# Weight products of 512 columns issued as halves of 256 columns

## The chip, the cores and the metric

The kernel runs on one core of a Trainium2 chip. The metric is the device time of one execution in microseconds (us). Before the change the median of three runs is 2204.62 us (2203.36 to 2204.85).

The core's engines work side by side: TensorE (PE in the profile) multiplies matrices, and its loading of the stationary operand, the weight load, is listed apart as PEld. VectorE is DVE, ScalarE is ACT, GpSimd is POOL, and SyncE (SP) issues most of the DMAs. A matmul writes to PSUM, an accumulation memory of banks that hold 512 float32 columns on each of 128 partitions. All other operands are in SBUF.

## The reference

The reference is a decoder trunk of two layers over 256 tokens of width 2048, in float32. Each layer is a mixer and a SwiGLU FFN, with an RMSNorm before and after each and the result added to the residual stream.

```python
for layer in range(DEPTH):                      # DEPTH = 2
    y = rms_norm(h, g[0])
    if layer % 2 == 0:
        y = sb_gla_mixer(y, w_in, w_gate_up, b_gate, gla_norm_gain, w_out)   # w_in 2048 x 6160, w_out 2048 x 2048
    else:
        y = s5_mixer(y, ..., w_glu)                                          # w_glu 2048 x 4096
    h = h + rms_norm(y, g[1])
    y = swiglu_ffn(rms_norm(h, g[2]), w_ffn_in[layer], w_ffn_out[layer])     # 2048 x 11264 and 5632 x 2048
    h = h + rms_norm(y, g[3])
```

The first mixer has stick-breaking attention and gated linear attention (GLA) between its two projections. The second has a diagonal state-space layer (S5), a GELU and a gated linear unit (GLU). Most of the arithmetic is in the six large weight matrices, and these are what the change is about.

## The kernel before, in words

**How a weight product is made.** The 256 tokens are two token blocks of 128. A weight matrix is cut into column blocks of 512, and each column block into units of 256 rows, that is two k-tiles of 128 rows. For a column block and a token block, TensorE sums over all k-tiles into one PSUM bank of 128 tokens x 512 columns. The stationary operand is 128 x 128 activations (k-tile by tokens), the moving operand 128 x 512 weights.

**The split into high and low parts.** To come close to float32 with TensorE's faster float32 type (F32R in the code), both operands are split into a high part, rounded to F32R, and a low part, the remainder. Three products of a k-tile are summed: high activation by high weight, high by low, low by high. In the code these are `xh`, `xl` for the activations and `hi`, `lo` for the weights; their tiles are whi and wlo for the weights and xh/xl, ah/al, og and os for the activations. A unit has two k-tiles, so a unit and a token block have six products. They are issued in the method `products` (lines 203 to 205), one k-tile after the other.

**Raw products.** The first eight units of the GLU aren't split. Their weights go in as float32 (`lo` is None, line 198), two products to a unit.

**How the weights come.** The class `Stream` has a plan of all weight chunks in the order of use (the method `plan`). A chunk is 512 rows x 512 columns, 1 MB, loaded by one DMA on SP's queue into one of 3 buffers (tile wraw). `convert` makes one unit from half a chunk: ScalarE copies 128 x 1024 elements into whi, and VectorE subtracts to get wlo; 5 buffers of each. `next` hands out units and converts a few ahead (the argument `ahead`, 3 or 4).

**The loops.** `linear` goes over column blocks, and in each over units; for each unit it calls `products` for token block 0 and then 1, and then `pump`, which issues some other work (attention, GLA, preparation of S5) between units, by a budget of estimated nanoseconds. After the last unit of a column block, ScalarE and VectorE read the two banks (`evac`). `pairwise` is the same for two column blocks by turns. The order in each engine's queue is the order in which the program calls, since the schedule is manual.

**Other matmuls that the prediction speaks of.** Line 734 is a small product of the GLA gate: 128 x 16 weights, F32R, moving operand 256 columns, 48 products in one accumulation. Line 810 is a float32 product of 128 x 128 by 128 columns in the GLA's levels. Lines 923 and 924 are float32 products of the attention with 256 and 128 columns. Line 1233 is a float32 product with 32 stationary columns in the preparation of S5; lines 480, 337 and 612 are transposes on TensorE.

Of the kernel before, what the change touches and what calls it, by code (L numbers as in the profile page):

```python
# [159 lines left out]
class Kern:  # L160
# [31 lines left out]
    def products(self, ps, acts, tb, u, part):  # L192
        hi, lo = part
        mm = self.nc.tensor.matmul
        if lo is None:
            for kk in range(2):
                k = 2 * u + kk
                mm(ps, lhsT=self.whole[k][:, tb * 128:(tb + 1) * 128], rhs=hi[:, kk, :], start=(k == 0), stop=(k == len(acts) - 1))  # L198
            return
        for kk in range(2):  # L200
            k = 2 * u + kk
            xh, xl = (a[:, tb * 128:(tb + 1) * 128] for a in acts[k])
            mm(ps, lhsT=xh, rhs=hi[:, kk, :], start=(k == 0), stop=False)  # L203
            mm(ps, lhsT=xh, rhs=lo[:, kk, :], start=False, stop=False)  # L204
            mm(ps, lhsT=xl, rhs=hi[:, kk, :], start=False, stop=(k == len(acts) - 1))  # L205


    def linear(self, blocks, acts, evac, opening=None, mid=None, hooks=None, spare=None):
# [497 lines left out]
    def gla(self, rs):  # L706
# [86 lines left out]
        yield from self.need(256)  # L793
        mix = self.got.pop(256)
        yield from products(S[1], mix, mix, 0, 128, lambda o, p: nc.vector.tensor_copy(o, p))
        for li, b in enumerate((64, 32, 16, 8, 4, 2, 1)):
            yield from self.need(2 * b + 1)
# [805 lines left out]
```

## Time and profile before

| What | Value |
|---|---|
| Median of the runs | 2204.62 us (2203.36 to 2204.85, 3 runs) |
| The profiled execution's own time | 2204.35 us |
| Its span, from the first to the last instruction | 2202.6 us |
| TensorE busy | 2159.6 us (98%), 10672 matmuls |
| Weight loads (PEld) | 1741.4 us (79%), 10672 |
| VectorE busy | 1319.5 us (60%) |
| ScalarE busy | 974.3 us (44%) |
| Mean granted clock of TensorE | 0.996 |
| DMA | 457.42 MB, mean 208 GB/s |

The page of the profile gives busy times, the groups of instructions and the chain of work that ended last. A row of a group reads: line, engine, operation, output and inputs, shapes, count, then the busy time and the mean of one in ns, then the idle time of the engine before them and what ended it. Successive matmuls overlap in the profile, so the mean duration of one is longer than the distance between two starts. A row of the timeline reads: start in us, length in us, engine, line, operation, output and inputs, shape, count; equal neighbours are merged into one row. A matmul's shape is written as weight rows x weight columns and then the moving operand. A row for one line of the program gives the shortest, the median and the longest duration in ns.

### The profile page before, as it was taken

The numbers are of one execution on the slowest core, as the hardware profiler recorded it, in microseconds if no ns is written. First come the engines' busy times: TensorE is split into PE (matmuls) and PEld (weight loads), VectorE is DVE, ScalarE is ACT, GpSimd is POOL, SyncE is SP. The second block draws the span as 40 slices with busy tenths as digits, with TensorE's granted clock in tenths as the row PEclk, the third lists the DMA queues.
The fourth block names the chain that finished last, engine by engine and source line by source line (L and its number), as shares of the span: only waits on it lengthen the run. The fifth ranks groups of instructions, "written<-read, shape, count | busy, mean of one in ns | idle before, by whom it ended". The sixth has DMA issues, their size and how long they took to land.

```text
span 2202.6 us, 26942 instructions
## 1 busy us (share of the span) xinstructions
PE 2159.6 (98%) x10672; PEld 1741.4 (79%) x10672; DVE 1319.5 (60%) x1913; ACT 974.3 (44%) x1222; POOL 7.1 (0%) x14
## 2 busy tenths in 40 slices
PE   8999999999999999999998899999999999999998
PEld 6888888788888888777786678878888888888886
DVE  4675654667777877875456864564544454444445
ACT  5454544463454444334344254464434444433433
POOL 0000000000000000000000000000000000000000
PEclk9999999999999999999999999999999999999999
DMA  7554454555687778988769865645555555555553
GB/s 230 171 176 156 159 173 155 206 190 175 202 268 236 241 221 267 300 275 275 238 214 349 305 209 185 213 170 176 195 183 191 191 173 190 174 206 174 191 172 134
DMA packets 261742, 457.42 MB, mean 208 GB/s; under 512 B 22736, under 2 KB 66016, under 8 KB 260720
## 3 DMA queue, kind: packets, MB, share of 16 engines
q1 hardware_dynamic: 260896, 450.99, 62.0%
q0 software_dynamic: 720, 4.72, 0.6%
q8 instruction: 83, 1.36, 0.2%
q14 instruction: 43, 0.35, 0.0%
HBM read 425.26 MB, written 30.41 MB: 207 GB/s over the span
## 4 chain that ended last, share of the span: by engine, by line
PE 94%; DVE 3%; ACT 1%; DMA 1%; issue 0%; SPq 0%; DVEq 0%; ACTq 0%
PE lin L203 29%; PE lin L205 29%; PE lin L204 29%; PE lin L198 1%; PE big L480 1%; DVE h L65 1%; DVE X L65 0%; PE big L810 0%; DVE wlo L65 0%; ACT xh L65 0%; PE big L1233 0%; PE big L205 0%; PE big L204 0%; PE big L203 0%; DVE xl L65 0%
## 5 line engine op out<-in xcount | busy, mean ns | idle before, releaser
L65 DVE TENSOR_TENSOR wlo<-wraw,whi 128x1024 fp32r<-128x1024 f32 x705 | 850.3, 1222 | 591.1 <-ACT whi L65 588.8
L65 ACT CAST whi<-wraw 128x1024 fp32r<-128x1024 f32 x705 | 725.3, 1051 | 670.7 <-PE lin L205 609.2
L203 PE MATMUL lin<-whi,xh 128*128 128x512 f32 x1984 | 790.6, 398 | 3.4 <-ACT xh L65 3.4
L204 PE MATMUL lin<-wlo,xh 128*128 128x512 f32 x1984 | 785.1, 396 | 3.0 <-DVE wlo L65 2.9
L205 PE MATMUL lin<-whi,xl 128*128 128x512 f32 x1984 | 784.9, 396 | 0.9 <-DVE xl L65 0.9
L203 PEld LDWEIGHTS lin<-whi,xh 128*128 128x128 f32 x1984 | 374.9, 189 | 91.2 <-ACT xh L65 4.0
L204 PEld LDWEIGHTS lin<-wlo,xh 128*128 128x128 f32 x1984 | 374.8, 189 | 90.4 <-DVE wlo L65 6.0
L205 PEld LDWEIGHTS lin<-whi,xl 128*128 128x128 f32 x1984 | 374.5, 189 | 88.7 <-DVE xl L65 2.2
L203 PE MATMUL lin<-whi,ah 128*128 128x512 f32 x680 | 270.0, 397 | 0.0
L205 PE MATMUL lin<-whi,al 128*128 128x512 f32 x680 | 268.9, 395 | 0.0
L204 PE MATMUL lin<-wlo,ah 128*128 128x512 f32 x680 | 268.9, 395 | 0.0
L203 PEld LDWEIGHTS lin<-whi,ah 128*128 128x128 f32 x680 | 128.1, 188 | 30.8 <-issue 1.2
L205 PEld LDWEIGHTS lin<-whi,al 128*128 128x128 f32 x680 | 128.1, 188 | 30.3
L204 PEld LDWEIGHTS lin<-wlo,ah 128*128 128x128 f32 x680 | 128.1, 188 | 30.0
L65 DVE SCALAR_TENSOR_TENSOR a<-lin,rs,a 128x512 f32<-128x512 f32 x44 | 31.0, 746 | 67.3 <-PE lin L205 67.3
L65 ACT ACTIVATE a<-lin,rs 128x512 f32<-128x512 f32 x44 | 27.9, 684 | 92.2 <-PE lin L205 92.2
L65 DVE TENSOR_TENSOR yg<-lin,yg 128x512 f32<-128x512 f32 x30 | 19.9, 687 | 52.1 <-PE lin L205 52.1
L65 ACT ACTIVATE junk<-yg 128x512 f32<-128x512 f32 x24 | 15.2, 632 | 74.1 <-DVE yg L65 74.1
L65 ACT CAST ah<-big 128x1024 fp32r<-128x1024 f32 x22 | 22.3, 1015 | 56.2 <-PE big L480 56.2
L65 DVE TENSOR_TENSOR al<-big,ah 128x1024 fp32r<-128x1024 f32 x22 | 26.9, 1223 | 17.1 <-ACT ah L65 17.1
L65 ACT ACTIVATE xh<-big,gT 128x128 fp32r<-128x128 f32 (+1 forms) x80 | 24.3, 394 | 21.5 <-PE big L337 16.9
L65 DVE SCALAR_TENSOR_TENSOR xl<-big,gT,xh 128x128 fp32r<-128x128 f32 (+1 forms) x80 | 24.5, 371 | 13.6 <-ACT xh L65 13.6
(323 smaller groups left out, 1287.1 us busy)
## 6 DMA issues: line engine op xcount, KB each, us to landing
wraw<-w_ffn_in SPq DMA_DIRECT2D x176, 1024.0 KB, 5.1
wraw<-w_ffn_out SPq DMA_DIRECT2D x88, 1024.0 KB, 5.5
wraw<-w_in SPq DMA_DIRECT2D x47, 1024.0 KB, 5.0
wraw<-w_glu SPq DMA_DIRECT2D x32, 1024.0 KB, 5.7
wraw<-w_out SPq DMA_DIRECT2D x16, 1024.0 KB, 5.1
e_d<-ed SPq DMA_DIRECT2D x64, 144.0 KB, 5.9
et<-e_d SPq DMA_DIRECT2D x16, 576.0 KB, 6.3
win_d<-win SPq DMA_DIRECT2D x32, 256.0 KB, 6.6
```

The lines of the kernel that those rows point to most:

```text
L65: return f(*a, **k)
L198: mm(ps, lhsT=self.whole[k][:, tb * 128:(tb + 1) * 128], rhs=hi[:, kk, :], start=(k == 0), stop=(k == len(acts) - 1))
L203: mm(ps, lhsT=xh, rhs=hi[:, kk, :], start=(k == 0), stop=False)
L204: mm(ps, lhsT=xh, rhs=lo[:, kk, :], start=False, stop=False)
L205: mm(ps, lhsT=xl, rhs=hi[:, kk, :], start=False, stop=(k == len(acts) - 1))
L480: nc.tensor.transpose(p[:, tb, i, :], a[:, tb, i * 128:(i + 1) * 128], self.ident)
```

## The change

The six products of a unit and a token block are no longer issued k-tile by k-tile over the whole bank. They are collected in a list in the same order, and issued for the left 256 columns of the bank and then for the right 256. Two products stay whole, 512 columns wide: the first of an accumulation, which starts it, and the last, which stops it. Every half has a matmul instruction of its own with its own weight load. The raw products (line 198) stay as they are, and no other line is touched.

```diff
+        terms = []
         for kk in range(2):
             k = 2 * u + kk
             xh, xl = (a[:, tb * 128:(tb + 1) * 128] for a in acts[k])
-            mm(ps, lhsT=xh, rhs=hi[:, kk, :], start=(k == 0), stop=False)
-            mm(ps, lhsT=xh, rhs=lo[:, kk, :], start=False, stop=False)
-            mm(ps, lhsT=xl, rhs=hi[:, kk, :], start=False, stop=(k == len(acts) - 1))
+            terms += [(xh, hi[:, kk, :]), (xh, lo[:, kk, :]), (xl, hi[:, kk, :])]
+        first, last = u == 0, 2 * u + 2 == len(acts)
+        if first:
+            x, w = terms.pop(0)
+            mm(ps, lhsT=x, rhs=w, start=True, stop=False)
+        final = terms.pop() if last else None
+        for c in (slice(0, 256), slice(256, 512)):
+            for x, w in terms:
+                mm(ps[:, c], lhsT=x, rhs=w[:, c], start=False, stop=False)
+        if last:
+            x, w = final
+            mm(ps, lhsT=x, rhs=w, start=False, stop=True)
```

## The prediction, made before the changed kernel was run

> **What bounds the kernel now.** I read the page from its engine line to the chain of waits and the groups, then TensorE's waits, then one long stretch of products in the timeline.
>
> ```profile
> span 2202.6 us, 26942 instructions
> PE 2159.6 (98%) x10672; PEld 1741.4 (79%) x10672; DVE 1319.5 (60%) x1913; ACT 974.3 (44%) x1222; POOL 7.1 (0%) x14
> ...
> PE 94%; DVE 3%; ACT 1%; DMA 1%; issue 0%; SPq 0%; DVEq 0%; ACTq 0%
> ...
> L65 DVE TENSOR_TENSOR wlo<-wraw,whi 128x1024 fp32r<-128x1024 f32 x705 | 850.3, 1222 | 591.1 <-ACT whi L65 588.8
> L65 ACT CAST whi<-wraw 128x1024 fp32r<-128x1024 f32 x705 | 725.3, 1051 | 670.7 <-PE lin L205 609.2
> L203 PE MATMUL lin<-whi,xh 128*128 128x512 f32 x1984 | 790.6, 398 | 3.4 <-ACT xh L65 3.4
> ```
>
> TensorE is busy for 98% of the span and makes 94% of the chain that ended last. The conversions of the weights (VectorE 1.22 us, ScalarE 1.05 us for each unit of 128x1024) feed it, and they sit idle for 591 and 671 us. So whatever changes TensorE's pace in the weight products changes the time almost one to one. The 398 ns of a product is not its price, because products overlap; the price is the distance between starts:
>
> ```profile
> 1811.87 0.48 PE L203 MATMUL lin<-whi,xh 128*128 128x512 f32 x1
> 1812.18 0.39 PE L204 MATMUL lin<-wlo,xh 128*128 128x512 f32 x1
> ...
> 1856.33 0.39 PE L205 MATMUL lin<-whi,xl 128*128 128x512 f32 x1
> ```
>
> ```profile
> L203 PE MATMUL lin<-whi,xh 128*128 128x512 f32 x64 | 25.4, 396 | 0.0
> L204 PE MATMUL lin<-wlo,xh 128*128 128x512 f32 x64 | 25.3, 395 | 0.0
> L205 PE MATMUL lin<-whi,xl 128*128 128x512 f32 x64 | 25.3, 395 | 0.0
> ```
>
> The second fence groups the stretch from 1811.87 us to 1856.57 us: 192 products and no idle time. From the second of them (1812.18) to the last (1856.33) are 190 distances in 44.15 us, or **232.4 ns for a product of 512 columns**. The granted clock was 1.00 there, and over most of the span:
>
> ```profile
> 1811.87:1856.57 44.70, 44.70 (x195) 36.27 (x194) 20.99 (x20) 18.64 (x19) 0.00 (x0) 1.00 0.56 188
> 465.00:1195.00 730.00, 730.00 (x3388) 586.92 (x3386) 505.58 (x862) 310.59 (x366) 0.29 (x1) 1.00 0.77 246
> ```
>
> (Columns: length, busy time of TensorE, of its weight loads, of VectorE, ScalarE and GpSimd, then granted clock, DMA share, GB/s.) VectorE's busiest long stretch, 465 to 1195 us, is 69% busy.
>
> **The change: how many instructions.** From the plan in the code: 96 units for w_in, 32 for w_out, 2 x 264 for the two FFNs, 56 for the GLU beside its 8 raw ones, 712 in all; times 2 token blocks and 6 products is 8544, which at 232.4 ns is 1986 us of the span. Left whole are the first product of each accumulation (92 column blocks x 2, less the 4 that begin raw: 180) and the last (184). So 8544 - 364 = **8180 products are split**: TensorE executes 10672 + 8180 = 18852 matmuls and as many weight loads. Every nanosecond that two halves cost over one whole is 8.2 us.
>
> **The price of a half** isn't in the trace: no matmul there has 256 columns of F32R data against 128 weight columns. These rows come closest (they write f32 for both types; the code tells which is F32R and which F32).
>
> ```profile
> 45.73 0.28 PE L734 MATMUL big<-xl,wlr_split 128*16 128x256 f32 x1
> ...
> 50.84 0.28 PE L734 MATMUL big<-xl,wlr_split 128*16 128x256 f32 x1
> ```
>
> ```profile
> L734 PE MATMUL big<-xl,wlr_split x16: 276/277/280, 45.7 to 50.8; 128*16 128x256 f32 x16
> ```
>
> The gate's low-rank product: F32R, 256 columns, each with its own weight load, accumulating into the same columns as a half will, but only 16 weight columns. One in three reads xl; sixteen of these span 15 x 3 = 45 distances in 5.11 us, or 113.6 ns. Two make 227.2, which is 5.2 ns *less* than 232.4.
>
> ```profile
> 118.42 1.79 PE big L810 x16
> ```
>
> ```profile
> L810 PEld LDWEIGHTS big<-qd,de x112: 187/192/193, 118.0 to 197.4; 128*128 128x128 f32 x112
> L810 PE MATMUL big<-qd,de x112: 273/276/276, 118.3 to 197.5; 128*128 128x128 f32 x112
> ```
>
> F32 of 128 columns lasts 276 ns against the 277 of L734, so it streams as long as a half, and here each has a full load of 128 weight columns. Sixteen take 1.79 us in the chain: 111.9 ns each. So a full load (192 ns long by itself) can hide under a stream of this length, and 111.9 is the fastest pace at which loads of this size are seen to follow one another. That is the lower bound: 2 x 111.9 - 232.4 = **-8.6 ns** a split.
>
> ```profile
> 1249.41 20.84 PE L198 MATMUL lin<-wraw,y 128*128 128x512 f32 x48 [0.63 <-DMA e<-e_d]
> ```
>
> ```profile
> L198 PE MATMUL lin<-wraw,y x64: 592/593/697, 1249.4 to 1281.8; 128*128 128x512 f32 x64
> L923 PE MATMUL big<-sqT,skT x16: 377/380/383, 239.9 to 338.9; 128*128 128x256 f32 x16
> ```
>
> ```profile
> 239.95 0.59 PE L923 MATMUL big<-sqT,skT 128*128 128x256 f32 x2
> 240.38 0.39 PE L924 MATMUL big<-sqT,skT 128*128 128x128 f32 x2
> ```
>
> What an instruction costs beside its columns: 593 - 380 = 213 ns is the stream of 256 F32 columns, 426 that of 512. The pace of L198 is (20.84 - 0.59) / 47 = 431 ns, 5 more; the pace of L923 is 0.43 / 2 = 215, 2 more. So **2 to 5 ns per instruction**, with 128 weight columns each time. I take 2.5, nearer the short instruction, since 2.5 also leaves room for the one late start inside L198's 48.
>
> The upper bound: 256 F32 columns stream in 213 ns, so 512 F32R columns, which last 393 to 396 ns against 380, stream in 213 or a little more. Were all of the 232.4 - 213 = 19.4 ns a price of the instruction, a split would cost **+19.4 ns**.
>
> The choice: of 232.4 I put 2.5 on the instruction and the rest on the 512 columns (0.449 ns each, where L734's are (113.6 - 2.5) / 256 = 0.434). Then a half is 117.4, two are 234.9, and a split costs **+2.5 ns**. I prefer it to L734's -5.2 because L734 lacks the 128 weight columns, and because a stream that costs less per column when it is short needs a reason that no row gives.
>
> The Trainium skill (TensorE: Matmul & The Clock Gate, Part 1, "Wait — 56ns, not 53.3ns?") gives a matmul N / 2.4 GHz plus about 2.5 ns, so 215.7 ns for 512 columns and, as an estimate from it, 109.2 for 256. The trace does not agree on the first (232.4, at a granted clock of 1.00), and the measurement decides. By that page's fixed term alone the change costs 8180 x 2.5 ns, 20 us.
>
> The same skill (Perfetto Trace Analysis, "Identifying the Most-Contended Engine") judges TensorE by the share of the time in weight-load slices, which speaks against this change: 79% now, and an estimate of 149% after, from 8180 more loads of 188 ns. L810's row shows that 192 ns slices follow each other every 111.9 ns, so slices overlap, and over 100% is no proof of a bound here.
>
> **The rest.**
>
> ```profile
> PE lin L204 <- DVE wlo L65: 2.9, 5, 0.8
> ```
>
> ```profile
> q8 instruction: 83, 1.36, 0.2%
> ...
> wraw<-w_ffn_in SPq DMA_DIRECT2D x176, 1024.0 KB, 5.1
> ```
>
> The first product with the low part starts up to 116 ns earlier after its unit's first one. That meets a late VectorE in 5 places (2.9 us in all): +0.6 us at most. whi is last read by the last product as before; wlo's last reading is the eleventh half of twelve, 116 ns later than now, under VectorE's 591 us of idle time: nothing. The last product stays whole, so what evacuates a bank waits for the same instruction. No load of weights is moved on SP's or POOL's queue. The instructions themselves come by DMA: 1.36 MB for 21344 of TensorE's is 64 bytes each, so 16360 more are 1.05 MB, 64 packets; no row shows TensorE waiting for them, and I take 0. If that cover were gone, each could cost what a load takes to land, 5.1 us: 326 us.
>
> Sum: 8180 x 2.5 ns = 20.5, + 0.6 = 21 us, against the profiled execution's own 2204.35 us (span 2202.6 and 1.75 around it; the median of the runs shown is 2204.62): **2225 us**. With 1 to 5 ns a split: 2212 to 2246.
>
> **Rivals.**
>
> *Short streams are cheaper (faster).* L734's pace holds with 128 weight columns too: 8180 x -5.2 = -43 us, **2162**. For it: the one row with F32R data of 256 columns; full loads can follow at 111.9, so they needn't stop it. Against it: 16 weight columns. It decides as soon as a half stays under 116.2 ns; at the floor of 111.9 it gives -70 us, 2134.
>
> *No change.* A half is just half, within 0.5 ns a split: **2204**. It needs the instruction's 2 to 5 ns to be offset by a cheaper stream.
>
> *The excess belongs to the switch of weights.* Part or all of the 19.4 ns comes with each change of 128 weight columns; a half then takes up to 126 ns: +159 us, **2363**, and half of it 2284. For it: 16 weight columns in L734 leave only 113.6 - 106.5 = 7.1 ns of excess, half of L923's 213 being 106.5. Against it are these rows:
>
> ```profile
> 863.75 0.40 PE L205 MATMUL lin<-whi,xl 128*128 128x512 f32 x1
> 864.07 0.64 PE L1233 MATMUL big<-et 128*32 128x128 f32 x16
> ```
>
> ```profile
> 864.07 0.38 PEld L1233 LDWEIGHTS big<-et 128*32 128x32 f32 x16 [0.36 <-PE lin L204]
> ```
>
> Beside the product at 863.75 no weights were loaded (the loads were idle for 0.36 us before 864.07), and it still lasted 0.40 us, like the others. So a load that runs beside a product doesn't seem to be what stretches it.
>
> *It doesn't do what it says*: the loads of a half can't keep up, or instructions come late, as priced above. Nothing in the trace speaks for it.
>
> **How the numbers follow.** Forecast 0.42; cheaper short streams 0.32; no change 0.12; the switch of weights 0.12; the last 0.02. A measurement of this kernel tells 0.2%, 4.4 us, from no change. Slower 0.42 + 0.12 + 0.02 less 0.01 for the low end of the forecast = 0.55; same 0.13; faster 0.32. The predicted time is 2225; its own range is 2212 to 2246. The range of 8 in 10 runs from 2150, below L734's price and above the floor of 2134, to 2320, most of the way to a whole excess at each switch.
>
> **What would show it.** In the changed profile: 18852 matmuls; the stretch of two FFN column blocks that took 44.70 us takes 45.2 by the forecast, 43.7 by L734's price, 48.3 by the switch; a half's distance is 117.4, 113.6 or 126 ns. VectorE's and ScalarE's busy times stay at 1319 and 974 us, and the waits of L198, L810 and the other stages stay as they are. I am wrong if a half takes under 116 ns, or if new idle time of TensorE appears within a unit.

## The result, and the profile after

The changed kernel takes **2238.56 us** (median of 4 runs, 2237.77 to 2241.25) against 2204.49 us before (4 runs): a ratio of 1.0158, 95% interval 1.0140 to 1.0175, so 34 us slower. The forecast was 2225 us, slower; its own range was 2212 to 2246.

The page of the changed kernel, in the same order as before; line 212 now issues the halves, 208 and 215 the first and last whole products.

```profile
span 2237.0 us, 43302 instructions
PE 2193.5 (98%) x18852; PEld 2142.3 (96%) x18852; DVE 1319.6 (59%) x1913; ACT 974.7 (44%) x1222; POOL 7.1 (0%) x14
...
q8 instruction: 147, 2.41, 0.4%
...
PE 40%; DVE 1%; ACT 1%; issue 0%; DVEq 0%; ACTq 0%
...
L65 DVE TENSOR_TENSOR wlo<-wraw,whi 128x1024 fp32r<-128x1024 f32 x705 | 850.0, 1222 | 614.8 <-ACT whi L65 609.9
L212 PE MATMUL lin<-wlo,xh 128*128 128x256 f32 x3968 | 1106.8, 282 | 3.1 <-DVE wlo L65 2.9
```

18852 matmuls, as counted. TensorE's busy time grew by 33.9 us and the span by 34.4: the loss lies within TensorE's own stream. Its idle time is 43.5 us (2237.0 - 2193.5) after 43.0. VectorE and ScalarE do the same work in the same time. 64 more packets bring 1.05 MB more of instructions. The chain that ended last is followed back over only 42% of the span on this page (PE 40%, where the page before had 94%), so this reading rests on the busy and idle times and not on the chain.

The same two FFN column blocks as before the change (window, then the two timeline rows that bound 374 distances between starts):

```profile
1841.22:1886.82 45.60, 45.60 (x379) 45.23 (x378) 20.99 (x20) 18.64 (x19) 0.00 (x0) 1.00 0.55 185
```

```profile
1841.43 0.28 PE L212 MATMUL lin<-wlo,xh 128*128 128x256 f32 x1
...
1886.70 0.28 PE L212 MATMUL lin<-whi,xl 128*128 128x256 f32 x1
```

45.60 us instead of 44.70 for 184 splits, with no gap in either. Of the 374 distances 8 belong to whole products (1.86 us at 232.4 ns); the other 366 share 43.41 us, **118.6 ns a half**. Over the kernel a split costs (2238.73 - 2204.35) us / 8180 = **4.2 ns**, from the two profiled executions.

### The profile page after: what moved, and what is told of

It is laid out like the page before. It is cut to its first block, busy times and chain, and to the rows that moved or that the text cites. A ratio compares the mean times of both kernels' runs of the same rounds, so it can differ in the third digit from the quotient of the medians.

```text
span 2237.0 us, 43302 instructions
## 1 busy us (share of the span) xinstructions
PE 2193.5 (98%) x18852; PEld 2142.3 (96%) x18852; DVE 1319.6 (59%) x1913; ACT 974.7 (44%) x1222; POOL 7.1 (0%) x14
## 5 line engine op out<-in xcount | busy, mean ns | idle before, releaser
L212 PE MATMUL lin<-wlo,xh 128*128 128x256 f32 x3968 | 1106.8, 282 | 3.1 <-DVE wlo L65 2.9
L212 PE MATMUL lin<-whi,xh 128*128 128x256 f32 x3722 | 1047.1, 283 | 0.0
L212 PE MATMUL lin<-whi,xl 128*128 128x256 f32 x3716 | 1041.4, 282 | 1.2 <-DVE xl L65 1.1
L212 PEld LDWEIGHTS lin<-wlo,xh 128*128 128x128 f32 x3968 | 747.7, 188 | 10.4 <-DVE wlo L65 4.9
L212 PEld LDWEIGHTS lin<-whi,xl 128*128 128x128 f32 x3716 | 699.9, 188 | 7.6 <-DVE xl L65 2.2
L212 PEld LDWEIGHTS lin<-whi,xh 128*128 128x128 f32 x3722 | 701.2, 188 | 2.5 <-issue 2.0
L212 PE MATMUL lin<-wlo,ah 128*128 128x256 f32 x1360 | 378.0, 281 | 0.0
L212 PE MATMUL lin<-whi,ah 128*128 128x256 f32 x1268 | 355.2, 282 | 0.0
L212 PE MATMUL lin<-whi,al 128*128 128x256 f32 x1268 | 354.4, 281 | 0.0
L212 PEld LDWEIGHTS lin<-wlo,ah 128*128 128x128 f32 x1360 | 256.1, 188 | 2.0
L212 PEld LDWEIGHTS lin<-whi,ah 128*128 128x128 f32 x1268 | 240.2, 189 | 1.0 <-issue 1.0
L212 PEld LDWEIGHTS lin<-whi,al 128*128 128x128 f32 x1268 | 238.6, 188 | 2.0
L208 PE MATMUL lin<-whi,xh 128*128 128x512 f32 x123 | 50.2, 408 | 1.9 <-ACT xh L65 1.8
L215 PE MATMUL lin<-whi,xl 128*128 128x512 f32 x126 | 49.8, 395 | 0.0
L212 PE MATMUL lin<-whi,og 128*128 128x256 f32 x210 | 38.7, 280 | 0.0
```

What stands on the lines that cost most here:

```text
L208: mm(ps, lhsT=x, rhs=w, start=True, stop=False)
L212: mm(ps[:, c], lhsT=x, rhs=w[:, c], start=False, stop=False)
L215: mm(ps, lhsT=x, rhs=w, start=False, stop=True)
```

## The experiments

Ten kernels ran in three groups; before took 2205.05, 2205.61 and 2205.90 us beside them.

**1. The order of the halves.** The twelve half products are the same; left and right of each product now follow each other, so that the same columns of the bank come again after two distances instead of one.

```diff
-        for c in (slice(0, 256), slice(256, 512)):
-            for x, w in terms:
+        for x, w in terms:
+            for c in (slice(0, 256), slice(256, 512)):
```

> Both halves of a product are issued one after the other (left, right) instead of six left and then six right; same instructions, same loads. If the price of 4.2 ns a split (34.2 us / 8180) belongs to the instruction, or to the weight load, the order doesn't matter: 2238 us, within 5. If it comes from adding into the same 256 columns again after 118 ns, alternating takes it away: near 2205 us and a distance of about 116 ns.

Measured: 2238.53 us, ratio 1.0152 (1.0135 to 1.0169). The order has no part in it, and adding into the same 256 columns again after 118 ns shows no cost.

**2. Half the splits.** Only token block 1 in halves.

```diff
-        for c in (slice(0, 256), slice(256, 512)):
+        for c in (slice(0, 256), slice(256, 512)) if tb else (slice(0, 512),):
```

> Only token block 1 is issued in halves, block 0 whole: 4090 splits instead of 8180. With a price of each split, whatever its cause: half of 34 us, 2222 us. If it were a bound that two engines or queues reach only when all products are halves (instructions that arrive too late, loads that can't keep up), less than half: under 2215 us.

Measured: 2219.91 us, ratio 1.0066 (1.0049 to 1.0083), 14.3 us slower. The interval, 11 to 18 us, holds half of the whole loss (17) and nothing of a threshold: the loss grows with the number of splits.

**3. Other widths.** The split at 320, 384 and 288 instead of 256. This asks two things: whether a piece's time is a line in its columns, and from which width the weight loads decide.

```diff
-        for c in (slice(0, 256), slice(256, 512)):
+        for c in (slice(0, 320), slice(320, 512)):
```

> The split at column 320 instead of 256: pieces of 320 and 192 columns. Price of the instruction (a line through 232.4 ns for 512 and 118.4 for 256 columns: 0.445 ns a column and 4.4 ns): the piece of 320 takes 147 ns; that of 192 would stream in 90 but can't be faster than the 111.9 ns at which full weight loads follow one another, so 259 a split, about 2420 us. If the halves of 256 were already set by the weight loads, the loads take about 118 here, the piece of 192 stays at 118, and the split is 265 ns, about 2470 us.

> Pieces of 384 and 128 columns. The line through 512 columns (232.6 ns) and 256 (118.4 ns), 0.446 ns a column and 4.4 ns an instruction, which the piece of 320 met (147.0), gives 175.5 ns for 384. The piece of 128 streams in about 61 ns and is held by the weight loads at 111 ns as the piece of 192 was: 286.5 a split, about 2645 us. If the price of an instruction isn't constant but the columns cost more in a long stream, the piece of 384 lies off the line.

> Pieces of 288 and 224 columns, to see from which width the weight loads decide. By the line the piece of 288 takes 132.8 ns and that of 224 would take 104.3, under the 111 ns of the loads: 243.8 a split, about 2297 us. If loads and stream disturb each other before that, the piece of 224 takes more than 113 ns.

Measured: 2411.79, 2640.77 and 2301.32 us, one execution each. Timeline of the split at 320, one token block's end and the next one's beginning:

```profile
1908.54 0.31 PE L212 MATMUL lin<-whi,xl 128*128 128x320 f32 x1
1908.69 0.31 PE L212 MATMUL lin<-whi,xh 128*128 128x320 f32 x1
1908.84 0.31 PE L212 MATMUL lin<-wlo,xh 128*128 128x320 f32 x1
1908.99 0.31 PE L212 MATMUL lin<-whi,xl 128*128 128x320 f32 x1
1909.13 0.25 PE L212 MATMUL lin<-whi,xh 128*128 128x192 f32 x1
1909.22 0.27 PE L212 MATMUL lin<-wlo,xh 128*128 128x192 f32 x1
1909.34 0.28 PE L212 MATMUL lin<-whi,xl 128*128 128x192 f32 x1
...
1909.78 0.33 PE L212 MATMUL lin<-whi,xh 128*128 128x320 f32 x1
```

The four distances from 1908.54 to 1909.13 are 147.5 ns each; the line said 146.9. The first piece of 192 takes 90 ns (1909.13 to 1909.22): its own load had run under the long piece before it. The five others, 1909.22 to 1909.78, take 112 ns each, though they would stream in 90. Timeline of the split at 384:

```profile
2084.15 0.39 PE L212 MATMUL lin<-whi,xh 128*128 128x384 f32 x1
2084.38 0.34 PE L212 MATMUL lin<-wlo,xh 128*128 128x384 f32 x1
2084.56 0.34 PE L212 MATMUL lin<-whi,xl 128*128 128x384 f32 x1
...
2085.26 0.22 PE L212 MATMUL lin<-whi,xh 128*128 128x128 f32 x1
2085.32 0.28 PE L212 MATMUL lin<-wlo,xh 128*128 128x128 f32 x1
...
2085.88 0.39 PE L212 MATMUL lin<-whi,xh 128*128 128x384 f32 x1
```

From 2084.56 to 2085.26 are four distances of 175 ns for 384 columns (line: 175.5); the first piece of 128 takes 60 ns, and the five after it 112 each. What the first saves is lost again behind the five: the long piece that follows them takes 230 ns (2084.15 to 2084.38) instead of 175. Six splits so take 1.73 us (2084.15 to 2085.88), 288 ns each, where 286.5 was expected. Timeline of the split at 288:

```profile
1821.62 0.28 PE L212 MATMUL lin<-wlo,xh 128*128 128x224 f32 x1
...
1822.18 0.30 PE L212 MATMUL lin<-whi,xh 128*128 128x288 f32 x1
1822.32 0.29 PE L212 MATMUL lin<-wlo,xh 128*128 128x288 f32 x1
...
1822.98 0.27 PE L212 MATMUL lin<-whi,xh 128*128 128x224 f32 x1
```

Five pieces of 224 take 112 ns each (1821.62 to 1822.18), and five of 288 take 132 (1822.32 to 1822.98; line: 132.8). So pieces of 128, 192 and 224 columns run at one pace, and that is the pace of the weight loads. Issuing a load and a product is not what takes 111 ns: the sixteen pairs of L1233, with 32 weight columns, take 0.64 us in the prediction's row, 40 ns each at most. The price of the whole agrees: (2411.79 - 2205.05) / 8180 = 25.3 ns a split where 26.4 was worked out, 53.2 for 54.1, and 11.7 for 11.4 at 288. With 128 weight columns, the time of a product is thus **4.4 ns and 0.446 ns a column**, and never under about 111 ns in a row. The line is drawn through 512 and 256 columns; 384, 320 and 288 test it, and lie within 1 ns of it. A half of 256, at 118, lies above that floor; the loads don't set it.

The Trainium skill (TensorE: Matmul & The Clock Gate, "LDWEIGHTS (loading the stationary operand)") puts a load at its columns over 1.2 GHz; an estimate from it is 107 ns for 128 columns, and the floor of 111 to 112 ns agrees with it to 5 ns. The load's own duration does not agree: the rows of loads in experiment 4 last 188, 134 and 94 ns for 128, 64 and 16 columns, each some 81 ns more than an estimate from that rule (107, 53 and 13).

**4. Narrow weights.** In all products but the first and last of an accumulation only 16 or 64 of 128 tokens are computed, in halves and, with 16, also whole.

```diff
-                mm(ps[:, c], lhsT=x, rhs=w[:, c], start=False, stop=False)
+                mm(ps[0:16, c], lhsT=x[:, 0:16], rhs=w[:, c], start=False, stop=False)
```

> Halves as in the change, but with 16 weight columns (16 of 128 tokens) in all products except the first and last of an accumulation; the other tokens' sums are left out. Price of the instruction alone: distance stays 118.4 ns, 2238 us. If 128 weight columns (loading them or computing with them) are what makes a half slower than the gate's product: 113.6 ns, about 2160 us.

> The same with 64 weight columns (64 of 128 tokens; the others' sums are left out). Price of the instruction: 118.4 ns, 2238 us. If the full load sets the pace of a half, a load of half the length frees it as much as 16 columns do: the same distance as with 16. If the cost grows with the active columns: halfway, about 116 ns and 2200 us.

> Whole products of 512 columns with 16 weight columns (16 of 128 tokens; the others' sums are left out) in all but the first and last of an accumulation. The halves with 16 weight columns took 114.7 ns against 118.4 with 128. If the weight columns change the price of an instruction (3.7 ns): 232.6 - 3.7 = 228.9 ns, about 2175 us. If they change the rate of the stream: 232.6 - 7.4 = 225.2 ns, about 2144 us.

| Weight columns | Halves, us | Whole, us | A split costs |
|---|---|---|---|
| 128 | 2238.56 | 2204.49 | +4.2 ns |
| 64 | 2218.19 | not run | |
| 16 | 2177.96 | 2191.63 | -1.7 ns |

(The cost is the difference over 8180; the rows of 16 and 64 are one execution each.) With 16 weight columns the same split is a *gain* of 13.7 us. A half loses 60.6 us / 16360 = 3.7 ns by narrower weights, a whole product 12.9 us / 8180 = 1.6 ns. So the 128 weight columns cost 7.4 ns on two halves and 1.6 on a whole, and this turns the sign. Neither form of the expectation holds: the effect is neither one sum per instruction (the whole would lose 3.7) nor one per column (the whole would lose 7.4). Nor is it a load that has to be done in time, by the halves with 64 columns, which should then run like those with 16. Weight loads of the three kernels with halves, 128, 64 and 16 columns:

```profile
L212 PEld LDWEIGHTS lin<-wlo,xh 128*128 128x128 f32 x3968 | 747.7, 188 | 10.4 <-DVE wlo L65 4.9
```

```profile
L212 PEld LDWEIGHTS lin<-wlo,xh 128*64 128x64 f32 x3968 | 532.8, 134 | 14.0 <-DVE wlo L65 5.6 <-issue 0.3
```

```profile
L212 PEld LDWEIGHTS lin<-wlo,xh 128*16 128x16 f32 x3968 | 373.9, 94 | 93.9 <-DVE wlo L65 5.6 <-issue 0.3
```

A load of 64 columns is 54 ns shorter than one of 128, yet it brings back only (2238.56 - 2218.19) us / 16360 = 1.2 of the 3.7 ns. In proportion to the load's length (54 of 94 ns) or to the weight columns (64 of 112) it would be 2.1.

**5. Zero weights.** Whether the time of a column depends on what is multiplied.

```diff
-        self.nc.scalar.copy(hi, raw)
-        self.nc.vector.tensor_sub(lo, raw, hi.bitcast(F32))
+        self.nc.scalar.activation(hi, raw, AF.Identity, scale=0.0)
+        self.nc.vector.tensor_sub(lo, hi.bitcast(F32), hi.bitcast(F32))
```

> The kernel before with weights made zero on the way (ScalarE scales by 0, VectorE subtracts a tile from itself), so all split products move zeros; the raw products keep their weights. If the 0.446 ns a column is a rate of the stream that doesn't depend on the data: 232.6 ns, 2205 us. If it comes from the load of computing with data: near the 213 ns that 256 float32 columns stream in plus 4, about 217 ns and 2075 us.

> The changed kernel with the same zero weights. If nothing depends on the data: 118.4 ns, 2238 us. If the rate does and the price of the instruction doesn't: about 217 / 2 + 2 = 111 ns, at the 111 ns floor of the weight loads, about 2115 us, so a split costs 4 to 5 ns there too.

Measured: 2204.47 and 2236.63 us, one execution each. The same group of whole products, before and with zeros:

```profile
L204 PE MATMUL lin<-wlo,xh 128*128 128x512 f32 x1984 | 785.1, 396 | 3.0 <-DVE wlo L65 2.9
```

```profile
L204 PE MATMUL lin<-wlo,xh 128*128 128x512 f32 x1984 | 784.3, 395 | 3.1 <-DVE wlo L65 2.9
```

785.1 us before, 784.3 with zeros. Whether the weights are zero has no part in the 0.446 ns a column, and a split costs 3.9 ns with zeros too. What was zero is the moving operand; the activations that come from the residual stream were not.

## Why the prediction was right, by its own steps

**The bound and the count** held. TensorE's pace in the weight products is the whole effect, 8180 products were split, and the other engines' times didn't move.

**The sign** hung on one choice: that the gate's product (113.6 ns) was no price for a half, because it has 16 weight columns. The runs with narrow weights confirm that: at 16 columns a half comes down to an average 114.6 ns (118.3 - 3.7, where 118.3 is half of 232.4 + 4.2), near L734's 113.6, and the split gains. The rival "short streams are cheaper" described a real effect, for narrow weights, and on the average falls for full ones.

**The size** is the step that was off. The term "2.5 ns per instruction", chosen from 2 to 5, measured 4.2 over the kernel and 4.4 as the constant of the line; the stretch of two FFN column blocks took 45.60 us and not 45.2, and a half 118.6 ns and not 117.4. With 4.4 the sum would have been 36 us, 2240. The two rows from which 2 to 5 were read say less than that. L198 from its second product on:

```profile
1249.92 20.33 PE L198 MATMUL lin<-wraw,y 128*128 128x512 f32 x47
```

That is (20.33 - 0.59) / 46 = 429 ns, 3 more than the stream's 426: the rest of the 5 came from the one late start, 0.51 us between the first product (1249.41) and the second. The 215 of L923 is half of 0.43 us, and since times are printed to 0.01 us it can be off by up to 5 ns, more than the 2 read from it. So the float32 rows said about 3 (2229 us), and the halves cost 4.2; where the difference comes from is not known. That 2239 lies inside the range is in part luck, since its upper end, 5 ns a split, came from the late start. Behind the size stands a simplification: one constant for each instruction, whatever the weights' width. At 128 columns the line is straight, and that suffices for this change; at 16 the two points, 114.6 and 230.8 (232.4 - 1.6), leave no positive constant.

**The rest.** The 0.6 us for an earlier need of the low parts didn't come: `L212 <- DVE wlo` waits 2.9 us in 5 places, as L204 did. The page of waits of the changed kernel:

```profile
PE lin L212 <- DVE wlo L65: 2.9, 5, 0.8
```

Instructions grew by the 64 packets worked out, and TensorE waits for none that the profile shows.

**The other rivals.** No change: out, the interval begins at 1.0140. The excess at the switch of weights: its size is out, since 19.4 ns a switch would give a half of 126 ns and pieces of 320 and 384 off the line; but weights matter more in a half than in a whole, as it supposed. The argument against it from the product beside which nothing was loaded was about a whole product, where the weights' width moves only 1.6 ns, and read a duration (0.40 us) where the price is a distance. Loads that can't keep up: not at 256 columns, but at 224. The Trainium skill (Perfetto Trace Analysis, "Identifying the Most-Contended Engine") judges how near TensorE is to its limit by the share of time in weight-load slices, beside the arithmetic done against the peak. By 96%, with overlapping slices counted once, there would be next to no room. The trace agrees only in part: loads in a row could go at 111 ns, and the halves run at 118.

**What stays open** is why 128 weight columns lengthen a half by 3.7 ns and a whole product by 1.6. It is not the weights' values, and not a load that comes too late; neither the load's length nor the number of active columns fits in proportion, and the two were not varied apart from each other. Every product here also has a load of its own, so no run tells whether the 4.4 ns belong to the matmul or to its load.

## What to carry to other kernels

Cutting a product into halves adds a matmul and a weight load for the same columns; where TensorE is the bound, price it by the distance between starts and not by durations, which here were 282 and 396 ns for 118 and 232. With this type and 128 weight columns, loads set the pace below some 240 columns (111 ns less 4.4, at 0.446 a column; an estimate between the 256 and 224 that ran), and each column left out of a piece is lost. A price read from a product with narrow weights may not even have the right sign.

## What was not expected of the hardware

The distance between starts is not one value with noise. It stands in patterns that hold for a stretch and differ between stretches. Two stretches of the halves with 16 weight columns, timeline rows with 13 and 9 equal distances:

```profile
800.09 0.28 PE L212 MATMUL lin<-whi,xl 128*16 128x256 f32 x1
...
801.65 0.28 PE L212 MATMUL lin<-whi,xh 128*16 128x256 f32 x1
```

```profile
1727.75 0.28 PE L212 MATMUL lin<-wlo,xh 128*16 128x256 f32 x1
...
1728.77 0.28 PE L212 MATMUL lin<-wlo,xh 128*16 128x256 f32 x1
```

120.0 ns in the one, 113.3 in the other, for the same instruction shapes. The 114.6 above is a mean over such stretches, so the 3.7 ns that narrow weights save is a mean too, and not the price of each instruction. With 128 weight columns most stretches stand near 118.6, but not all; a stretch of the output projection in the changed kernel, 18 distances:

```profile
359.75 0.28 PE L212 MATMUL lin<-wlo,og 128*128 128x256 f32 x1
...
361.79 0.28 PE L212 MATMUL lin<-wlo,og 128*128 128x256 f32 x1
```

2.04 us / 18 = 113.3 ns, with full weight loads. So 128 weight columns don't forbid the fast pace; they make it rare. Were all halves at 113.3, two would take 226.6, and by this estimate the change would gain 47 us (5.8 ns on 8180) instead of losing 34. What puts a stretch into one pattern or another was not found, and no version that beats the kernel before came out of it.
